# Matmul with batch norm over all rows: two column blocks stored by GpSimd's converting transfers, and the row pieces of two more chunks in halves

## The chip, the cores and the metric

The kernel runs on one core of one Trainium2 chip. The metric is the device time of one execution in microseconds. Before the change it is 205.8 us (median of 3 runs, 205.72 to 206.01).

The engines are named as in the profile: PE is TensorE (PEld is its weight load), DVE is VectorE, ACT is ScalarE, POOL is GpSimd, SP is SyncE, which here only issues DMAs. POOL also issues DMAs, and only those that it issues change the data type on the way.

## The reference

```python
def reference(x, weight, gamma, beta, eps):      # x 16 x 512 x 1024, weight 1024 x 768, f32
    y = np.matmul(x, weight)
    mean = np.mean(y, axis=(0, 1), keepdims=True)
    var = np.var(y, axis=(0, 1), keepdims=True)
    y_norm = (y - mean) / np.sqrt(var + eps)
    return (gamma * y_norm + beta).astype(np.float32)
```

x is 8,192 rows of 1,024 values, 33.5 MB. The output is 8,192 rows of 768 columns, 25.2 MB in f32. Each column is normalised over all rows, so nothing of a column can be stored before the matmuls of that column are done for all rows.

## The kernel before

**Tiles.** The rows are cut into 16 chunks of 512 (`C`). The 768 columns are cut into 6 column tiles of 128 (`NT`), numbered `nt` 0 to 5. Tiles 0 and 1 are the first group (`GA`), computed with rows on the partitions. Tiles 2 to 5 are computed turned, with columns on the partitions and 512 rows per PSUM bank, so their output has to be turned back before it is stored. The "third tile" of the title is `nt = 2`.

**Load stage (about 2 to 100 us).** POOL issues the loads of x (L402) into an SBUF area named `ring`; they convert f32 to bf16. DVE turns each chunk (L434, L427) into `xT_sb`. PE computes the first group of each chunk (L509) and the other tiles of the early chunks (L574). From about 100 us on, everything is in SBUF, and the remaining column tiles run from there at 8 matmuls (L574) for each tile and chunk.

**One column tile and chunk.** PE fills a PSUM bank (`y_ps`, 8 banks in all). DVE reads it for the statistics (L710). ACT casts it to bf16 into `y_sb` (L714), after which the bank is free. For most of tile 2, ACT does both (L719, L723). Where the moving operand is still interleaved, some chunks are first copied into plain order (`x_pl`, L546), by ACT or by DVE: those of chunks 12 to 15 for tile 4 are given to whichever of the two the planner finds free.

**First group, stored by rows (`rows_out`).** A row piece is multiplied by the scale on DVE (L936), the shift is added (L941, on POOL except for five pieces that `ADDED` gives to DVE), and SP stores it (L945). A piece is 4 row tiles of 128 rows (512 KB), except for chunks 0 and 1, which go in two pieces of 2 row tiles (256 KB).

**Tiles 2 to 4, stored in blocks of two chunks (`col_block`).** There are 8 blocks per tile, each 512 KB of output. There are four ways. `MODE` names the way of a block:

- `xact`: the block is normalised in place (L1022 on ACT for tile 2, L1025 on DVE else); SP issues a DMA transpose into a bf16 slot of `ring` (L1219); ACT casts it into an f32 slot (L1231); SP stores that (L1201).
- `xpool`: as far as the transpose the same; then POOL issues one DMA that reads the bf16 slot, converts, and writes the f32 output (L1225). No cast, no f32 slot, no store by SP. Before the change no block takes this way.
- `pe`: PE turns the block (L1043) between other matmuls, ACT copies it out of PSUM (L1209), SP stores (L1201). Tile 4 takes it.
- blocks named in `RAW` (0 and 2 of tiles 2 and 3; 0, 2 and 4 of tile 4, counted in chunks) skip `MODE`: they are transposed raw (L1105), scaled by DVE (L1173), shifted by POOL (L1177), stored by SP (L1181). For them the scale and shift of the tile are spread over the partitions by small copies (L1144: 4 gathers of 32 x 64 and 3 deals of 32 x 256 for each tile, which either POOL or ACT may do) and a copy into PSUM (L1157).

One block of tile 4 is held back to fill the gap before the last tile's scale is known (L1251, L1254).

**The end.** The last matmuls of tile 5 (L752) end its statistics (L759, L1307, L1310, L1322, L1323). DVE then normalises tile 5 (L1347), PE turns it (L1043), ACT copies it out (L1360), and SP stores 4.2 MB (L1363).

**What sets the order.** A planner (`arrange`) takes every task with its own guesses of costs and due times and writes out one fixed order for each engine and DMA queue; each queue then runs in that order and waits by semaphores. The planner also places slots in `ring`, so a slot can be used again only when the store or transpose that read it has landed. An edit of one block's way can therefore move other instructions, between engines too. The first column tile to be finished by `col_block` is tile 2.

Of the kernel before, what the change touches and what calls it, by code (L numbers as in the profile page):

```python
# [227 lines left out]
def kernel(  # L228
# [44 lines left out]
    XT, YB, SQ = C - EARLY, 29, 3  # L273
    ADDED = (0,6,16,28,40)
    PARTED, LATE, SINGLE = (4,5,7,8,9,10), (12,13,14,15), (2,3,6)
    MODE = {2:'xact',3:'xact',4:('pe',)*8}
    MODE = {nt: m if isinstance(m, tuple) else (m,) * (C // GY) for nt, m in MODE.items()}
    RAW, RAWADD, RAWDUE = {2:(0,2),3:(0,2),4:(0,2,4)}, {2:'POOL',3:'POOL',4:'POOL'}, {2:14.0,3:8.0,4:8.0}
    RING = 3 * CH // 32 * KQ // 2
# [75 lines left out]
    def task(prio, engines, emit, deps=(), lock=False, **kw):  # L355
        t = Task(prio, engines, emit, deps, **kw)
        t.lock = lock
        tasks.append(t)
        return t

    def dve(occ):
        return {"DVE": (occ, occ + 0.09)}

    def act(occ):
        return {"ACT": (occ, occ + 0.11)}
# [81 lines left out]
    for kind, n, *n1 in order:  # L447
# [24 lines left out]
        for i in range(rows // QR):  # L472
            c, q = divmod(m0 // QR + i, QPC)
# [9 lines left out]
        if rows % QR:  # L483
            t0 = rows // QR * QR // 32
            m1 = m0 + 32 * t0
            c, q = divmod(m1 // QR, QPC)
# [442 lines left out]
    def rows_out(c, s0, s1, k):  # L929
        due = S + 5.0 + 0.62 * k  # L930
        n = s1 - s0
        slot = Slot(rings, n * NA)

        def norm(eng):
            slot.o = piece(slot).rearrange("p (s n) -> p s n", n=NA)
            seq(nc.vector.tensor_mul(  # L936
                slot.o, y_row[c].y[:, s0:s1], aff[0][:, None, :].to_broadcast([P, n, NA])))

        def add(eng):
            row = sum1[:, 0:NA] if eng == "POOL" else aff[1]  # L940
            seq(ENG[eng].tensor_add(slot.o, slot.o, row[:, None, :].to_broadcast([P, n, NA])))  # L941

        def store(eng):
            m0 = c * CH
            seq(nc.sync.dma_start(  # L945
                out_flat[m0 + s0 * P:m0 + s1 * P, 0:NA].rearrange("(s p) n -> p s n", p=P), slot.o))

        keeps = [row_end[k][3] for k in row_end if k[0] == c]
        a = task(due, dve(0.3 * n), norm, [p0] + keeps, takes=[slot], uses=[y_row[c], a0_slot])
        b = task(due + 0.4, dve(0.3 * n) if k in ADDED else pool(0.59 * n), add, [a, p1 if k in ADDED else sh],  # L950
                 uses=[slot, a1_slot] if k in ADDED else [slot])
        task(due + 1.0, {"SP": (0.38, 0.4)}, store, [b], dma=n * NA * P * 4 / 1024 / 365.0 * 1.024,
             uses=[slot])

    k = 0
    for c in range(RC):
        for s0_, s1_ in ((0, 2), (2, 4)) if c < 2 else ((0, 4),):
            rows_out(c, s0_, s1_, k)
            k += s1_ - s0_

# [57 lines left out]
    def norm(nt, c, n=1):  # L1018
        def emit(eng):
            part = y(nt, c, n)  # L1020
            if eng == "ACT":
                seq(nc.scalar.activation(  # L1022
                    part, part, AF.Identity, bias=shift[:, nt:nt + 1], scale=scale[:, nt:nt + 1]))
            else:
                seq(nc.vector.tensor_scalar(  # L1025
                    part, part, scale[:, nt:nt + 1], shift[:, nt:nt + 1],
                    op0=ALU.mult, op1=ALU.add))
        return emit

    def turn_block(prio, nt, m0, count, deps, uses):  # L1030

        bank = Slot(banks)
        todo = []

        def step():
            if not todo:
                o_ps = psum.tile([P, count, P], bf16, tag="b")
                bank.tile = o_ps
                for s in range(count):
                    c, i = divmod(m0 // P + s, RT)  # L1040
                    todo.append((o_ps[:, s], y(nt, c)[:, i * P:(i + 1) * P]))
            dst, src = todo.pop(0)
            seq(nc.tensor.transpose(dst, src, ident))  # L1043

        def emit(eng):
            for _ in range(emit.task.count):
                step()

        emit.step = step
        t = task(prio, pe(0.0555 * count), emit, deps, takes=[bank], uses=uses)  # L1050
        emit.task = t
        turns[t] = [count, count]
        return t, bank
# [136 lines left out]
    def col_block(nt, c, due, fin_task, held=False):  # L1190
# [12 lines left out]
        a = task(due, act(1.144) if nt == GA else dve(0.45), norm(nt, c, GY), [fin_task] + keeps, nt > GA, uses=[yslot])  # L1203
        if MODE[nt][c // GY] == "pe":
            b, bank = turn_block(due + 0.5, nt, m0, count, [a], [yslot])
# [11 lines left out]
        def xbar(eng):  # L1217
# [3 lines left out]
        b = task(due + 0.5, {"SP": (1.4, 1.4)}, xbar, [a], dma=XBAR,  # L1221
                 takes=[t_slot] + ([slot] if MODE[nt][c // GY] == "xact" else []), uses=[yslot])
        if MODE[nt][c // GY] == "xpool":
            def store_x(eng):
                seq(nc.gpsimd.dma_start(dst(), t_slot.o))  # L1225
# [185 lines left out]
```

## Time and profile before

| | |
|---|---|
| time, median of 3 | 205.8 us (205.72 to 206.01) |
| the profiled execution | 205.96 us, of which the span shown is 204.2 us and 1.76 us lie around it |
| granted TensorE clock | mean 0.975; 1.00 in each stretch looked at between 112 and 190 us |
| busy: PE, DVE, ACT, POOL | 191.0, 158.7, 146.6, 126.1 us |
| HBM read, written | 36.71 MB, 25.17 MB |

How to read it: the page's second part cuts the span in 40 slices of 5.1 us, each digit a busy share in tenths. A row of groups gives the line, engine, operation, out<-in, shapes and count, then busy us and mean ns of one, then the idle time just before these instructions and who ended it. In a timeline a row starts with its start in us and its length in us. In a table of windows, the columns are the stretch, then busy us (and count) of PE, PEld, DVE, ACT and POOL, the granted clock, the mean busy share of the DMA engines and the GB/s moved.

### The profile page before, as it was taken

How to read it: one execution, taken by the hardware profiler on the slowest of the kernel's cores; microseconds unless marked ns; L12 is line 12 of the kernel's file. 1: busy time of each engine (PE TensorE's matmuls, PEld its weight loads, DVE VectorE, ACT ScalarE, POOL GpSimd, SP SyncE). 2: the span in 40 equal slices, each digit the busy share in tenths (PEclk: the TensorE clock that was granted, in tenths of full speed). 3: DMA queues.
4: the chain of work that ended last, by engine and by line, in shares of the span. 5: the costliest groups of instructions: out<-in, count | busy, mean ns of one | idle time of the engine just before them, and what ended most of it. 6: DMA issues, size and time to landing. Idle time of an engine off the chain costs nothing.

```text
span 204.2 us, 3509 instructions
## 1 busy us (share of the span) xinstructions
PE 191.0 (94%) x1210; PEld 116.3 (57%) x1210; DVE 158.7 (78%) x248; ACT 146.6 (72%) x261; POOL 126.1 (62%) x151
## 2 busy tenths in 40 slices
PE   7989999999999999999999999999999999996910
PEld 3467565656588888777875444444444445544810
DVE  4031979989999999969989998977999777937900
ACT  2001461468989999999978766999998969856950
POOL 7776964777399989997403999289616502850000
PEclk9999999999999999999999999999999999999685
DMA  4999999999999999999689999899999999999998
GB/s 73 168 200 196 181 196 196 196 198 197 189 194 197 197 199 194 196 197 195 93 187 214 334 339 336 242 306 326 316 291 201 334 322 244 347 343 310 309 347 249
DMA packets 98562, 48.74 MB, mean 239 GB/s; under 512 B 24304, under 2 KB 98032, under 8 KB 98544
## 3 DMA queue, kind: packets, MB, share of 16 engines
q0 software_dynamic: 34624, 18.36, 65.3%
q1 hardware_dynamic: 63920, 30.16, 53.7%
q8 instruction: 9, 0.15, 0.3%
q14 instruction: 9, 0.07, 0.1%
HBM read 36.71 MB, written 25.17 MB: 303 GB/s over the span
## 4 chain that ended last, share of the span: by engine, by line
PE 86%; ACT 3%; DMA 3%; POOL 2%; issue 1%; ACTq 0%; DVE 0%; POOLq 0%
PE y_ps L574 54%; PE y_ps L509 24%; PE y_ps L813 4%; ACT o_sb L1360 3%; DMA ring<-in_x_dram 3%; PE o_ps L1043 1%; POOL ring L402 1%; POOL w_sb L386 1%; PE y_ps L752 1%; PE a_ps L902 1%; PE o_ps L1073 0%; ACTq L1406 0%; PE idle_ps L590 0%; PE tot_ps L870 0%; ACT ring L1251 0%
## 5 line engine op out<-in xcount | busy, mean ns | idle before, releaser
L574 PEld LDWEIGHTS <-w_sb 128*128 128x128 bf16 x520 | 50.3, 97 | 57.6
L574 PE MATMUL y_ps<-xT_sb,w_sb 128*128 128x512 bf16 (+1 forms) x272 | 59.3, 371 | 0.0
L574 PE MATMUL y_ps<-x_pl,w_sb 128*128 128x512 bf16 x248 | 57.4, 379 | 0.0
L402 POOL DMA_DIRECT2D ring<-in_x_dram x76 | 47.3, 626 | 14.3 <-DMA ring<-in_x_dram 5.3
L509 PE MATMUL y_ps<-w_sb,xT_sb 128*128 128x256 bf16 x448 | 50.6, 273 | 0.7 <-DMA ring<-in_x_dram 0.6
L509 PEld LDWEIGHTS <-xT_sb 128*128 128x128 bf16 x448 | 43.5, 98 | 8.6 <-DVE xT_sb L434 2.1
L434 DVE STREAM_TRANSPOSE xT_sb<-ring 128x1024 f32<-128x1024 f32 (+1 forms) x29 | 31.2, 1112 | 14.1 <-DMA ring<-in_x_dram 14.0
L710 DVE BATCH_NORM_STATS2 stats<-y_ps 128x6 f32<-128x512 f32 x46 | 30.9, 687 | 8.6 <-PE y_ps L574 8.4
L546 ACT COPY x_pl<-xT_sb 128x1024 bf16<-128x1024 bf16 x34 | 34.8, 1063 | 1.7 <-DVE xT_sb L434 1.7
L714 ACT CAST y_sb<-y_ps 128x512 bf16<-128x512 f32 x51 | 28.7, 595 | 8.5 <-DVE stats L710 4.7
L941 POOL TENSOR_TENSOR ring<-ring,sum 128x1024 f32<-128x1024 f32 (+1 forms) x11 | 23.7, 2180 | 15.0 <-ACT y_ps L723 10.8
L658 ACT ACTIVATE sq_sb<-y_ps 128x512 f32<-128x512 f32 x28 | 16.4, 611 | 16.9 <-PE y_ps L509 16.4
L665 POOL TENSOR_TENSOR sum<-sum,sq_sb 128x512 f32<-128x512 f32 x20 | 25.6, 1280 | 3.1 <-ACT sq_sb L658 1.9
L661 DVE TENSOR_TENSOR sum<-y_ps,sum 128x512 f32<-128x512 f32 x28 | 18.9, 675 | 6.4 <-ACT sq_sb L658 5.3
L671 ACT CAST y_sb<-y_ps 128x512 bf16<-128x512 f32 x28 | 16.3, 593 | 8.3 <-DVE sum L661 8.0
L1177 POOL TENSOR_TENSOR ring<-ring,sum 128x1024 f32<-128x1024 f32 x7 | 17.1, 2469 | 4.5 <-issue 2.7
L936 DVE TENSOR_TENSOR ring<-y_sb,a_ps 128x1024 f32<-128x1024 bf16 (+1 forms) x16 | 16.7, 1080 | 0.1
L1144 POOL COPY sum<-sum 32x256 f32<-32x256 f32 (+1 forms) x17 | 5.5, 325 | 16.0 <-ACT sum L1144 9.2
L1043 PE MATMUL o_ps<-ident,y_sb 128*128 128x128 bf16 x104 | 13.7, 249 | 1.6 <-DVE y_sb L1347 1.5
L427 DVE STREAM_TRANSPOSE xT_sb<-ring 128x2048 bf16<-128x2048 bf16 x6 | 13.5, 2290 | 0.2 <-DMA ring<-in_x_dram 0.2
L1231 ACT CAST ring<-ring 128x1024 f32<-128x1024 bf16 x12 | 12.6, 1060 | 0.6 <-DMA ring<-y_sb 0.5
L590 PE MATMUL idle_ps<-idle_sb 128*128 128x512 f32 x18 | 10.5, 741 | 1.5 <-DVE idle_sb L316 1.5
(104 smaller groups left out, 154.9 us busy)
## 6 DMA issues: line engine op xcount, KB each, us to landing
out_dram<-ring SPq DMA_DIRECT2D x37, 512.0 KB, 3.5
ring<-in_x_dram POOLq DMA_DIRECT2D x52, 256.0 KB, 8.9
out_dram<-o_sb SPq DMA_DIRECT2D x6, 512.0 KB, 4.8
ring<-in_x_dram POOLq DMA_DIRECT2D x16, 128.0 KB, 5.8
w_sb<-in_weight_dram POOLq DMA_DIRECT2D x8, 192.0 KB, 6.2
out_dram<-ring SPq DMA_DIRECT2D x6, 256.0 KB, 3.1
ring<-in_x_dram POOLq DMA_DIRECT2D x4, 192.0 KB, 7.8
out_dram<-o_sb SPq DMA_DIRECT2D x3, 256.0 KB, 2.6
```

The source lines that it names most:

```text
L402: bi = seq(nc.gpsimd.dma_start(x_bf[32 * i:32 * i + 32], src[:, :, KQ * i:KQ * (i + 1)]))
L434: seq(nc.vector.transpose(dst, src[:, :, jw0:jw1]))
L509: seq(nc.tensor.matmul(y_ps[:, s], x_of(c, jw, e, t * P, (t + 1) * P), w_sb[:, jw, e, 0:NA], start=(s == 0 and jw == 0 and e == 0), stop=( ...
L546: seq(nc.scalar.copy(dst, pairs) if eng == "ACT" else ENG[eng].tensor_copy(dst, pairs))
L574: seq(nc.tensor.matmul(y_ps, w_sb[:, jw, e, nt * P:(nt + 1) * P], moving(c, jw, e, q0 * QR, q1 * QR, parted), start=(jw == 0 and e == 0 an ...
L661: seq(nc.vector.tensor_add(sum1, slot.tile[:, 0:n], sum1))
L665: seq(ENG[eng].tensor_add(acc, acc, state["sq"][:, 0:n]))
L710: seq(nc.vector.bn_stats(dst, slot.tile))
L714: seq(nc.scalar.copy(y(nt, c), slot.tile))
L936: seq(nc.vector.tensor_mul(slot.o, y_row[c].y[:, s0:s1], aff[0][:, None, :].to_broadcast([P, n, NA])))
L941: seq(ENG[eng].tensor_add(slot.o, slot.o, row[:, None, :].to_broadcast([P, n, NA])))
L1177: seq(ENG[eng].tensor_add(slot.o, slot.o, row[:, None, :].to_broadcast([P, n, P])))
```

## The change

Two edits. In `MODE`, which names the way for each of the 8 blocks of a tile, blocks 2 and 4 of tile 2 (chunks 4 and 5, 8 and 9) become `xpool`; blocks 0 and 1 of that tile are raw either way. In the loop over row pieces, chunks 2 and 3 of the first group go in two pieces each as chunks 0 and 1 do.

```diff
-    MODE = {2:'xact',3:'xact',4:('pe',)*8}
+    MODE = {2:('xact','xact','xpool','xact','xpool','xact','xact','xact'),3:'xact',4:('pe',)*8}
...
     for c in range(RC):
-        for s0_, s1_ in ((0, 2), (2, 4)) if c < 2 else ((0, 4),):
+        for s0_, s1_ in ((0, 2), (2, 4)) if c < 4 else ((0, 4),):
             rows_out(c, s0_, s1_, k)
             k += s1_ - s0_
```

The code of the `xpool` way, there already:

```python
        if MODE[nt][c // GY] == "xpool":
            def store_x(eng):
                seq(nc.gpsimd.dma_start(dst(), t_slot.o))

            task(due + 1.2, {"POOL": (0.93, 0.93)}, store_x, [b], dma=1.69, uses=[t_slot])
```

In the order that is built from the two kernels, PE's instructions are the same, one for one. The others differ from about the seventh row piece of DVE on:

| line | what | before | after |
|---|---|---|---|
| L1231 | cast 128 x 1024, ACT | 12 | 10 |
| L1201 | store 512 KB, SP | 16 | 14 |
| L1225 | converting store, POOL | 0 | 2 |
| L936 | multiply 128 x 1024 / 128 x 512, DVE | 12 / 4 | 10 / 8 |
| L941 | add 128 x 1024 / 128 x 512, POOL | 9 / 2 | 7 / 6 |
| L945 | store 512 / 256 KB, SP | 12 / 4 | 10 / 8 |
| L546 | copy to plain order, ACT / DVE | 34 / 6 | 31 / 9 |
| L1144 | gathers 32 x 64, ACT / POOL | 4 / 8 | 8 / 4 |
| L1144 | deals 32 x 256, ACT / POOL | 0 / 9 | 9 / 0 |

The two L1225 stand on POOL with one whole L941 add between them and one behind them, ahead of four L1177.

## The prediction

> **What bounds the kernel now.** First the page: span, busy times, granted clock, and the groups that the edit touches.
>
> ```profile
> span 204.2 us, 3509 instructions
> PE 191.0 (94%) x1210; PEld 116.3 (57%) x1210; DVE 158.7 (78%) x248; ACT 146.6 (72%) x261; POOL 126.1 (62%) x151
> ...
> PEclk9999999999999999999999999999999999999685
> ...
> L574 PE MATMUL y_ps<-xT_sb,w_sb 128*128 128x512 bf16 (+1 forms) x272 | 59.3, 371 | 0.0
> L402 POOL DMA_DIRECT2D ring<-in_x_dram x76 | 47.3, 626 | 14.3 <-DMA ring<-in_x_dram 5.3
> L546 ACT COPY x_pl<-xT_sb 128x1024 bf16<-128x1024 bf16 x34 | 34.8, 1063 | 1.7 <-DVE xT_sb L434 1.7
> L941 POOL TENSOR_TENSOR ring<-ring,sum 128x1024 f32<-128x1024 f32 (+1 forms) x11 | 23.7, 2180 | 15.0 <-ACT y_ps L723 10.8
> L1231 ACT CAST ring<-ring 128x1024 f32<-128x1024 bf16 x12 | 12.6, 1060 | 0.6 <-DMA ring<-y_sb 0.5
> ```
>
> PE is busy for 94% of the span, L574 has no idle time before it, and the clock is full until slice 38. The chain that ended last is 86% PE. So from about 100 us to the last matmul (186.65 us in the chain) the time is PE's own, and no relief on ACT, POOL or SP shortens it. Whatever the edit saves there is worth nothing; it can only cost, by making PE wait, or change the end behind PE. The table of windows shows the DMA engines over both stretches:
>
> ```profile
> 172.00:174.00 2.00, 2.00 (x17) 1.16 (x16) 1.41 (x3) 2.00 (x4) 0.00 (x0) 1.00 0.70 213
> 174.00:176.00 2.00, 2.00 (x16) 1.07 (x14) 2.00 (x4) 2.00 (x4) 1.59 (x1) 1.00 1.15 346
> ...
> 188.00:190.00 2.00, 1.33 (x15) 0.82 (x16) 1.96 (x7) 1.48 (x5) 0.00 (x0) 1.00 0.89 269
> 190.00:192.00 2.00, 2.00 (x24) 1.74 (x23) 2.00 (x8) 2.00 (x4) 0.00 (x0) 0.66 0.84 253
> ```
>
> 346 GB/s is full rate. They last run short at 172 to 174 us, are then full to about 187, and are short again at 188 to 192: the backlog is gone before the last tile's stores begin (L1363, 189.35 us). The tail hangs on the end of PE, not on the queue. Last, the timeline and the waits of the engine that stands closest behind PE, DVE:
>
> ```profile
> 145.85 0.54 DVE L992 SCALAR_TENSOR_TENSOR tmp<-mv,gamma_sb 128x1 f32<-128x1 f32 x1
> ...
> 153.58 0.70 DVE L710 BATCH_NORM_STATS2 stats<-y_ps 128x6 f32<-128x512 f32 x1 [0.44 <-PE y_ps L574]
> ...
> 160.56 0.70 DVE L710 BATCH_NORM_STATS2 stats<-y_ps 128x6 f32<-128x512 f32 x1 [1.03 <-PE y_ps L574]
> ...
> 164.02 0.70 DVE L710 BATCH_NORM_STATS2 stats<-y_ps 128x6 f32<-128x512 f32 x1 [0.78 <-PE y_ps L574]
> ...
> 168.09 0.53 DVE L1025 TENSOR_SCALAR y_sb<-y_sb,scale,shift 128x1024 bf16<-128x1024 bf16 x1
> ```
> ```profile
> DVE ring L1173 <- DMA out_dram<-ring: 0.8, 1, 0.8
> ```
>
> The brackets are DVE's rest time: 0.44 + 1.03 + 0.78 = 2.25 us, in which it waits for PE and so has caught up. At 168.62 us the L1025 ends that I take the first hosted transpose (PEld L1043, 169.00 us) to need: 0.38 us more. So DVE may lose about 2.6 us between 150 and 164 us before PE feels it. The last line shows the way in: L1173, in DVE's fixed order, already once waits for a store to free its place in `ring`, and behind it stand the statistics (L710), then ACT's cast (L714), then the bank that PE wants.
>
> **The change, part by part.**
>
> *Two casts and two SP stores go.* ACT loses 2 x 1.06 = 2.1 us (L1231), SP two issues of about 0.4 us. Off PE's path: nothing gained in time.
>
> *Two converting stores come, on POOL.* No such store is in this trace. Issue: the nearest row is L402, 626 ns for 512 pieces; this one has 1,024, so 0.63 to 1.25 us, and I take 0.95. Transfer: the x loads move and convert as many values (131,072 each) and the GB/s row holds 196 in the load stage, so 262,144 B / 196 GB/s = 1.34 us; a plain store of the same bytes in the same 1,024 pieces of 512 B takes 524,288 B / 346 GB/s = 1.51 us. If pieces set the price it is 2 x 1.34 = 2.68 us. I take 1.5, the plain store's, as its written side is the same; the range keeps 1.34 to 2.68. By that value the DMA engines do the same work as before.
>
> *Who stands behind them.* POOL waits in order for the transpose (median 4.4 us to landing); behind it are one add (L941) after each, then the L1177. Behind those adds SP's L945 waits (its waits on L941 are 11.5 us in 9 already), and behind L945 the next transposes. POOL has cover: 3.58 us of idle before the L941 at 131.22 us, and the copies leave it. Two issues and about 1 us of waiting on landings come to 2.9 us: inside that.
>
> *Small copies change sides.* POOL loses 4 gathers of 0.23 and 9 deals of 0.39 us, 4.4 us; ACT gains 4 x 0.24 + 9 x about 0.38 (the 128 x 256 copy L1157) = 4.4 us, and gives 3 copies L546 (3 x 1.06 = 3.2 us) to DVE. ACT in sum: -2.1 + 4.4 - 3.2 = -0.9 us. It is busy for all of 128 to 144 us, and five L714 stand in one row at 161.54 us, so up to five of 8 banks were full then; one more holds the spread scale. Two free banks at 1.73 us each are some 3 us of cover (an estimate from these rows), and ACT's net load falls.
>
> *DVE gets more.* Three L546 at 0.69 us = 2.1 us, between 137 and 160 us, against room of 2.6: 0.5 us is left. This is the tightest place. If that cover is gone, each further us on DVE is one on PE.
>
> *Halves.* Two L936 of 1.21 become four of 0.68: +0.3 us on DVE near 115 us, covered by the 0.93 us that DVE idles at 125.7. Two L941 of 2.38 become four of 1.27: +0.3 us on POOL. SP issues two stores more, 2 x 0.37 us, waiting on POOL anyway. The store after the first half starts some 1.2 us sooner; DMA has room there, so nothing.
>
> *The tail.* SP's list behind 165 us holds the same stores of tile 4. A store that slips past 172 us costs 1.51 us of backlog, of which (346 - 269 + 346 - 253) / 346 x 2 = 0.98 us is idle room at 188 to 192. With two stores off SP's queue I expect none to slip.
>
> Sum: PE 0, tail 0. The profiled 205.96 us (204.2 + 1.76 around it) is 0.16 above the median; in the median's terms 205.8 + 0 = 205.8.
>
> **The rivals.**
>
> *Slower, the converting store is dear.* At 2.68 us two of them push the stores that free `ring` by 2 x 1.17 = 2.3 us, L1173's wait grows by that, DVE has 0.5 to spare, PE loses 1.8: 207.6 us. Halfway, about 206.7. It decides from 0.25 us extra on each. For it: the wait in the last fence. Against: loads of x convert at full read rate, and other stores can pass in the meantime. Chance 0.24.
>
> *Slower, DVE is held by POOL.* L992 took 0.54 us above, 0.16 elsewhere, and ended at 146.39, when POOL's L1177 ended (146.36). If a moved L546 starts beside an add of 2.38 us it may stand for all of it: 2.4 - 0.5 = 1.9 us, 207.7; half of it, 206.5. Against: in 143 to 154 us only one of six L546 ran long (0.92 for 0.69), though the adds were there. The Trainium skill (SBUF — State Buffer, "Who interferes with whom") states this as an exclusive lock for the whole instruction, with issue order deciding who blocks; L992's end agrees. The same page, in "SBUF: two separate sides", speaks against the change itself: it says that descriptors of GpSimd's DMAs cannot be written while such a DVE operation runs. No run here shows it, since L402 has no such copy beside it; by its 620 against 3,100 ns (an estimate from that page) each issue would be 2.5 us longer. Chance of this rival 0.12, and 0.02 for PE being held elsewhere.
>
> *Faster.* Only the idle 0.98 us at 188 to 192 could be won, if less backlog let the tail's stores begin sooner: 205.8 - 0.5 = 205.3, at most 204.8. Against: L1360 begins at 188.96 behind DVE and PE, and the first store follows it. Chance 0.10.
>
> *The change doesn't do what it says.* The built order holds both L1225, so no.
>
> **How the numbers follow.** Forecast 0.52, dear store 0.24, port 0.12, elsewhere 0.02, faster 0.10. 0.2% (0.41 us) is about what a measurement of this kernel can tell from no change. So faster 0.10, same 0.52, slower 0.24 + 0.12 + 0.02 = 0.38. The forecast's own range is 205.5 to 206.1. For 8 in 10 I go up to 207.0, over the halfway values of both slower rivals, leaving out their upper ends, and down to 205.4.
>
> **What would show it.** Right: L574 still with 0.0 idle, the last L752 ending near 186.65, the rows at 188 to 192 as now; L1225 below 1.3 us of issue, landing about 4 us after issue; PE's waits without L1043 or L574. Wrong: idle on PE behind DVE or ACT at 140 to 175 us, a wait of L1173 on out_dram over 2 us (dear store), L546 over 1 us beside an add (port), or 346 GB/s through 188 to 192 (backlog).

## The result, and the profile after

| | before | after |
|---|---|---|
| time, median of 4 (same chip) | 205.76 us (205.67 to 206.01) | 208.30 us (208.19 to 208.59) |
| ratio | | 1.0124, 95% interval 1.0106 to 1.0141 |
| span of the profiled execution | 204.2 us | 206.6 us |
| end of the last matmul L752 | 186.65 us | 188.18 us |
| first store of tile 5 (L1363): issued, landed | 189.35, 191.53 us | 190.88, 193.99 us |

The change costs 2.5 us; the forecast of 205.8 us and the range up to 207.0 were wrong. In the span the loss has two parts: the matmuls end 1.53 us later, and the first store behind them takes 0.93 us longer to land (3.11 for 2.18 us). First two lines of the page before, the chain and the statistics on DVE, then the page after: span, engines, chain, the same statistics and the converting stores.

```profile
PE 86%; ACT 3%; DMA 3%; POOL 2%; issue 1%; ACTq 0%; DVE 0%; POOLq 0%
...
L710 DVE BATCH_NORM_STATS2 stats<-y_ps 128x6 f32<-128x512 f32 x46 | 30.9, 687 | 8.6 <-PE y_ps L574 8.4
```

```profile
span 206.6 us, 3520 instructions
...
PE 190.0 (92%) x1210; PEld 115.9 (56%) x1210; DVE 163.6 (79%) x253; ACT 147.1 (71%) x269; POOL 124.3 (60%) x142
...
PE 62%; DVE 12%; DMA 9%; ACT 8%; issue 2%; POOL 2%; ACTq 0%; DVEq 0%; POOLq 0%
...
L710 DVE BATCH_NORM_STATS2 stats<-y_ps 128x6 f32<-128x512 f32 x46 | 30.3, 684 | 4.0 <-PE y_ps L574 4.0
...
out_dram<-ring POOLq DMA_DIRECT2D x2, 512.0 KB, 5.6
```

PE's share of the chain has gone from 86% to 62%, DVE has entered with 12%. DVE is busy for 4.9 us more, and rests 4.0 us in front of L710 where it rested 8.4 us before. The two converting stores land 5.6 us after their issue (median). Next the timeline of DVE and POOL from the second converting store on; a row is start, length, engine, line.

```profile
136.64 0.91 POOL L1225 DMA_DIRECT2D out_dram<-ring  x1
...
136.71 4.38 DVE L546 COPY x_pl<-xT_sb 128x1024 bf16<-128x1024 bf16 x2
...
137.56 2.37 POOL L941 TENSOR_TENSOR ring<-ring,sum 128x1024 f32<-128x1024 f32 x1
...
142.90 2.35 POOL L1177 TENSOR_TENSOR ring<-ring,sum 128x1024 f32<-128x1024 f32 x1 [2.97 <-DVE ring L1173]
...
143.95 1.85 DVE L546 COPY x_pl<-xT_sb 128x1024 bf16<-128x1024 bf16 x1
...
147.60 2.37 POOL L1177 TENSOR_TENSOR ring<-ring,sum 128x1024 f32<-128x1024 f32 x1 [2.35 <-DVE ring L1173]
...
149.09 0.90 DVE L992 SCALAR_TENSOR_TENSOR tmp<-mv,gamma_sb 128x1 f32<-128x1 f32 x1
```

Two copies took 4.38 us. The first one's own record is 136.71 to 140.49 us: 3.78 us where a free copy takes 0.68, ending 0.56 us after POOL's add (139.93). The third took 1.85 us and ended 0.55 us after the L1177 beside it. Then L992 took 0.90 us, where it takes 0.16 alone, and ended with the next L1177. That is 3.1 + 1.2 + 0.7 = 5.0 us of DVE time lost in 13 us. What follows from it is in the timelines of DVE and PE and in the windows:

```profile
158.21 1.22 DVE L1173 TENSOR_TENSOR ring<-r_sb,a_ps 128x1024 f32<-128x1024 bf16 x1 [1.23 <-DMA out_dram<-ring]
...
170.14 0.53 DVE L1025 TENSOR_SCALAR y_sb<-y_sb,scale,shift 128x1024 bf16<-128x1024 bf16 x1
```
```profile
170.73 0.23 PE L1043 MATMUL o_ps<-ident,y_sb 128*128 128x128 bf16 x1 [1.50 <-DVE y_sb L1025]
```
```profile
148.00:150.00 2.00, 2.00 (x12) 0.88 (x10) 2.00 (x5) 2.00 (x5) 1.97 (x1) 1.00 0.00 0
...
174.00:176.00 2.00, 2.00 (x17) 1.17 (x16) 0.58 (x1) 1.98 (x5) 0.00 (x0) 1.00 0.72 216
...
188.00:190.00 2.00, 0.63 (x10) 0.44 (x8) 1.47 (x6) 1.66 (x5) 0.00 (x0) 1.00 1.10 333
190.00:192.00 2.00, 1.80 (x20) 1.13 (x20) 2.00 (x8) 1.50 (x5) 0.00 (x0) 1.00 1.00 302
```

The L1025 that the prediction names (168.09 us before) begins at 170.14, and PE stands for 1.50 us before its first hosted transpose. Between 148 and 150 us the DMA engines move nothing at all (316 GB/s before): SP stands at a store L1201 whose cast on ACT (L1231) ends only at 149.33 us, and ACT had waited 2.0 us for DVE between 141 and 146 us. The last short stretch lies at 174 to 176 us instead of 172 to 174, and at 188 to 192 us, where before had 269 and 253 GB/s, the queue is now busier.

### The profile page after: what moved, and what is told of

Same layout as the page of the kernel before. It is cut to its first block, busy times and chain, and to the rows that moved or that the text cites. A ratio compares the mean times of both kernels' runs of the same rounds, so it can differ in the third digit from the quotient of the medians.

```text
span 206.6 us, 3520 instructions
## 1 busy us (share of the span) xinstructions
PE 190.0 (92%) x1210; PEld 115.9 (56%) x1210; DVE 163.6 (79%) x253; ACT 147.1 (71%) x269; POOL 124.3 (60%) x142
## 4 chain that ended last, share of the span: by engine, by line
PE 62%; DVE 12%; DMA 9%; ACT 8%; issue 2%; POOL 2%; ACTq 0%; DVEq 0%; POOLq 0%
PE y_ps L574 34%; PE y_ps L509 21%; DMA w_sb<-in_weight_dram 6%; DVE stats L710 4%; PE y_ps L813 4%; ACT o_sb L1360 3%; DMA ring<-in_x_dram 3%; DVE x_pl L546 3%; DVE ring L1173 2%; PE o_ps L1043 2%; ACT x_pl L546 1%; DVE y_sb L1025 1%; ACT y_sb L714 1%; POOL ring L402 1%; ACT sum L1144 1%
## 5 line engine op out<-in xcount | busy, mean ns | idle before, releaser
L710 DVE BATCH_NORM_STATS2 stats<-y_ps 128x6 f32<-128x512 f32 x46 | 30.3, 684 | 4.0 <-PE y_ps L574 4.0
L546 ACT COPY x_pl<-xT_sb 128x1024 bf16<-128x1024 bf16 x31 | 31.8, 1055 | 2.0 <-DVE xT_sb L434 1.7
L941 POOL TENSOR_TENSOR ring<-ring,sum 128x1024 f32<-128x1024 f32 (+1 forms) x13 | 24.1, 1880 | 14.6 <-ACT y_ps L723 10.8
L1177 POOL TENSOR_TENSOR ring<-ring,sum 128x1024 f32<-128x1024 f32 x7 | 17.1, 2452 | 19.7 <-DVE ring L1173 15.6
L936 DVE TENSOR_TENSOR ring<-y_sb,a_ps 128x1024 f32<-128x1024 bf16 (+1 forms) x18 | 16.8, 972 | 0.0
L1043 PEld LDWEIGHTS <-y_sb 128*128 128x128 bf16 x104 | 8.8, 112 | 4.5 <-DVE y_sb L1025 2.0
L590 PE MATMUL idle_ps<-idle_sb 128*128 128x512 f32 x18 | 9.6, 685 | 1.5 <-DVE idle_sb L316 1.5
L1231 ACT CAST ring<-ring 128x1024 f32<-128x1024 bf16 x10 | 10.4, 1049 | 0.6 <-DMA ring<-y_sb 0.6
```

Source lines behind the costliest of these rows:

```text
L546: seq(nc.scalar.copy(dst, pairs) if eng == "ACT" else ENG[eng].tensor_copy(dst, pairs))
L710: seq(nc.vector.bn_stats(dst, slot.tile))
```

## The experiments

The theory after the result: DVE's copies L546 are **held** while POOL works (theory A). The rivals: DVE simply has too much work (B, **load**); the stores on POOL keep places of `ring` too long (C, **ring**). "Before" below is the kernel before, run on the same chip. The edits of experiments 1 to 4 are made in the changed kernel, those of experiment 5 in the kernel before. The second edit of experiment 1 takes the `xpool` blocks back, which leaves the kernel before with the halves.

**1. One part of the change alone.** The third tile is `nt` 2, the one with the `xpool` blocks.

```diff
-        for s0_, s1_ in ((0, 2), (2, 4)) if c < 4 else ((0, 4),):
+        for s0_, s1_ in ((0, 2), (2, 4)) if c < 2 else ((0, 4),):
```

> Only the first part of the change: blocks 2 and 4 of the third tile stored by GpSimd's converting transfers; the row pieces stay as before. Theory A (hold): a copy L546 on DVE that meets an add of POOL stands for as long as POOL works. The first L546 of the changed kernel (136.71 us, 3.78 us long) does not depend on the row halves, so A expects a copy of 3 us or more near 137 us again, PE's wait at L1043 of about 1.5 us, and 208.0 to 208.5 us. Theory B (load): DVE has too much work after 130 us, whoever disturbs it. Less work by 0.3 us without the halves: 207.9 to 208.3. Theory C (ring): the two stores keep places of ring too long, L1173 waits for them and DVE is late by that; the stores are the same, so 208.0 to 208.5. If the halves alone are at fault, 205.8.

Measured: 208.20 us, ratio 1.0104 (1.0067 to 1.0141). The first copy took 3.79 us again.

```diff
-    MODE = {2:('xact','xact','xpool','xact','xpool','xact','xact','xact'),3:'xact',4:('pe',)*8}
+    MODE = {2:'xact',3:'xact',4:('pe',)*8}
```

> Only the second part: row pieces of chunks 2 and 3 in halves, the third tile's blocks cast by ScalarE and stored by SP as before. A, B and C all expect 205.7 to 206.0 us, PE's last L752 ending near 186.65 us, and no copy L546 over 1 us. Above 206.5 the halves have a part in the loss.

Measured: 206.21 us, ratio 1.0006 (0.9991 to 1.0021); L752 ended at 186.39 us. The halves cost nothing that can be measured; the loss belongs to the two blocks. A, B and C remain.

**2. The same work in a form that is not held.** Same order on every engine; three copies are written as a maximum over one element.

```diff
-    pending = []
+    pending, one_port = [], [1, 1, 1]
...
-                seq(nc.scalar.copy(dst, pairs) if eng == "ACT" else ENG[eng].tensor_copy(dst, pairs))
+                seq(nc.scalar.copy(dst, pairs) if eng == "ACT" else nc.vector.tensor_reduce(dst, pairs[:, :, :, None], axis=mybir.AxisListType.X, op=ALU.max) if eng == "DVE" and one_port and one_port.pop() else ENG[eng].tensor_copy(dst, pairs))
```

> The changed kernel with its first three DVE copies L546 (at 136.7, 140.4 and 143.9 us) written as a reduction over one element, which gives the same values. The order of every engine is unchanged. The new form costs more by itself: an estimate of 1.1 to 1.2 us each from L936 (1.20 us for 1,024 values of a partition), against 0.69 for an unhindered copy, so +1.3 us of work on DVE. A (hold): if the hold is a matter of the copy's form and the new form is free of it, the three take 1.1 to 1.2 us each although POOL's adds run beside them, DVE wins 6.3 - 3.5 = 2.8 us against the changed kernel, PE's idle time before L1043 at 169 us goes, and the time is 205.8 to 206.3. If the new form is held too, the first stands for 3.8 us again and the time is about 208.3 or more. B (load): DVE carries 1.3 us more work than in the changed kernel: 208.3 to 209.5. C (ring): the stores and L1173's places are the same: 207.5 to 208.5, and L1173 waits for out_dram as long as before or longer.

Measured: 205.94 us, ratio 0.9995 (0.9978 to 1.0012). Its timeline:

```profile
136.75 2.33 DVE L546 TENSOR_REDUCE x_pl<-xT_sb 128x1024 bf16<-128x1024 bf16 x2
...
137.60 2.37 POOL L941 TENSOR_TENSOR ring<-ring,sum 128x1024 f32<-128x1024 f32 x1
...
140.88 2.39 POOL L1177 TENSOR_TENSOR ring<-ring,sum 128x1024 f32<-128x1024 f32 x1 [0.91 <-DVE ring L1173]
...
141.93 1.20 DVE L546 TENSOR_REDUCE x_pl<-xT_sb 128x1024 bf16<-128x1024 bf16 x1
```

Each takes 1.20 us with POOL's add beside it. Without a hold these three would cost DVE 1.6 us more than three free copies of 0.68 us, and yet the whole loss is gone. B and C fall: the load was larger, and the stores were the same and landed as late (5.3 and 5.9 us after their issue). The Trainium skill (SBUF — State Buffer, "Who interferes with whom") says of this reduction that on trn2 it never contends with GpSimd, and of copies that they can; both agree with these rows.

**3. Which POOL instruction holds the copy.** First the add behind the second L1225 is left out:

```diff
-            seq(ENG[eng].tensor_add(slot.o, slot.o, row[:, None, :].to_broadcast([P, n, NA])))
+            seq(ENG[eng].tensor_add(slot.o, slot.o, row[:, None, :].to_broadcast([P, n, NA]))) if k != 52 else None
```

> The changed kernel without the last L941 on POOL, the one that stands behind the second L1225 (137.56 us): the shift of one row piece (chunk 13, first half) is left out. Which POOL instruction holds the copy at 136.71 us: the issue of L1225 (136.64 to 137.55 us), the add behind it (137.56 to 139.93 us), or both? In the changed kernel the copy ended 0.56 us after the add. If the issue holds DVE as well, the copy now ends 0.56 us after the issue, about 1.4 us long. If only adds hold it, and the copy lost its place to the add that came later, it takes 0.69 us. A (hold): DVE gains 2.4 or 3.1 us against the changed kernel, and the time falls to 205.8 to 206.5. B (load): DVE has no instruction less; 208.3. C (ring): only the store of the row piece comes 2.4 us sooner; 207.5 to 208.3.

Measured: 206.16 us, ratio 1.0011 (0.9994 to 1.0027).

```profile
136.43 1.23 POOL L1225 DMA_DIRECT2D out_dram<-ring  x1
...
136.51 1.65 DVE L546 COPY x_pl<-xT_sb 128x1024 bf16<-128x1024 bf16 x2
```

The first copy took 0.68 us, the second 1.05, ending 0.49 us after the issue; the issue itself took 1.23 instead of 0.91 us. So an issue and a copy do get in each other's way, but for tenths of a us. Yet this copy began 13 ns after an add had ended, that of the changed kernel in the same ns; it could have been a matter of who asks first. So the add ahead was shortened, to let the copy ask in the middle of the issue:

```diff
-            row = sum1[:, 0:NA] if eng == "POOL" else aff[1]
-            seq(ENG[eng].tensor_add(slot.o, slot.o, row[:, None, :].to_broadcast([P, n, NA])))
+            row, m = sum1[:, 0:NA] if eng == "POOL" else aff[1], 3 if k == 48 else n
+            seq(ENG[eng].tensor_add(slot.o[:, :m], slot.o[:, :m], row[:, None, :].to_broadcast([P, m, NA])))
```

> The changed kernel with the last L941 but one on POOL (134.34 to 136.71 us) shortened to three quarters: the shift of a quarter of one row piece (chunk 12) is left out. It ends about 0.55 us sooner, at 136.15 us, and the second L1225 issues from about 136.1 to 137.0 us; the copy L546 on DVE still asks at 136.7 us, now in the middle of that issue, with the full add L941 behind it at 137.0 to 139.4 us. Two ways in which the hold could work. H1: whoever asks while POOL still computes loses its turn to POOL's next add too; in the changed kernel the copy began in the same hundredth of a us in which an add ended. Then the copy now gets through in 0.7 us, makes the issue longer by some 0.3 us (1.23 for 0.91 us without the add behind it), and the time is 205.8 to 206.3. H2: an issue followed by an add keeps the copy out anyway. Then the copy ends 0.56 us after the full add, at about 139.9 us, 3.2 us long, and the time is 207.5 to 208.5.

Measured: 207.09 us, ratio 1.0050 (1.0030 to 1.0070).

```profile
136.13 0.91 POOL L1225 DMA_DIRECT2D out_dram<-ring  x1
...
136.74 3.84 DVE L546 COPY x_pl<-xT_sb 128x1024 bf16<-128x1024 bf16 x2
...
137.06 2.37 POOL L941 TENSOR_TENSOR ring<-ring,sum 128x1024 f32<-128x1024 f32 x1
```

The first copy stood from 136.74 to 139.98 us, 3.24 us, until 0.56 us after the end of the add, which began 0.31 us later than it. That is H2: a copy that meets the issue also waits for the add right behind the issue. The time, 207.09 us, lies between H1's and H2's: PE lost nothing here (L752 at 186.64 us; L1173 waited 0.2 us for its place in `ring`, not 1.23), and the loss of 1.1 us is all behind PE. Experiment 5 takes that up.

**4. Versions in which no copy meets an issue with an add behind it, nothing left out.** The add given to DVE:

```diff
-    ADDED = (0,6,16,28,40)
+    ADDED = (0,6,16,28,40,52)
```

> The changed kernel with the add behind the second L1225 given to DVE (one more number in ADDED), nothing left out. The scheduler then puts 1.2 us more work on DVE, ahead of the first copy L546, and the copies one by one between the L710. Hold theory: POOL has nothing to compute between the issue's end (about 137.5 us) and its first L1177 (about 142 us), so the first two copies take 0.7 to 1.0 us; a third that meets an L1177 takes up to 1.9. DVE loses some 2 us to holds instead of 5 and has 1.2 us more work: 205.8 to 206.8. Load theory (fallen already in the run with the three reductions): 209. If the ring's places mattered, no change against the changed kernel, 208.3.

Measured: 206.23 us, ratio 1.0011 (0.9992 to 1.0029). A second run gave the profile:

> The same kernel as in the run before with the add on DVE, for its profile. Its time was 206.23 us there, so PE should have at most 0.3 us of idle time before L1043 at 169 us. Hold theory: the two copies near 138 to 140 us take 0.7 to 1.0 us each since POOL has only the issue of L1225 beside them and nothing to compute behind it; the third meets an L1177 and takes up to 1.9 us. If one of the first two takes over 2 us, the time is explained otherwise than by the hold.

```profile
136.28 0.91 POOL L1225 DMA_DIRECT2D out_dram<-ring  x1
...
136.85 0.83 DVE L546 COPY x_pl<-xT_sb 128x1024 bf16<-128x1024 bf16 x1
...
138.20 0.67 DVE L546 COPY x_pl<-xT_sb 128x1024 bf16<-128x1024 bf16 x1
```

Again a copy asks in the middle of the issue; with no add behind it, it is through after 0.83 us. The third, beside an L1177, took 1.89. Next, the planner. In both kernels it already keeps a DVE task marked `lock`, which these copies are, apart from POOL's adds (`port`), but not from a DMA that POOL issues. Now it is told that the issue of a converting store occupies POOL as an add does:

```diff
-        elif e == "POOL" and not t.dma:
+        elif e == "POOL" and (t.lock or not t.dma):
...
-        if e == "DVE" and t.lock or e == "POOL" and not t.dma:
+        if e == "DVE" and t.lock or e == "POOL" and (t.lock or not t.dma):
...
-            task(due + 1.2, {"POOL": (0.93, 0.93)}, store_x, [b], dma=1.69, uses=[t_slot])
+            task(due + 1.2, {"POOL": (0.93, 0.93)}, store_x, [b], True, dma=1.69, uses=[t_slot])
```

> The changed kernel, but the scheduler counts the issue of a converting store as a time in which POOL holds DVE's copies off. Nothing is left out; it then lays out POOL, DVE and ACT anew: seven small copies L1144 go back to POOL, and the first DVE copy L546 comes behind the second L1177 instead of at 136.7 us. Hold theory: no copy stands beside the adds behind L1225, so no copy is longer than 1.9 us, PE does not wait for L1025 at 169 us, 205.7 to 206.3. If it is as fast as the kernel before, the stores themselves cost nothing. A result above 207 would mean that the hold is only moved, to the copies beside the L1144 and L1177 on POOL.

Measured: 206.04 us, ratio 1.0001 (0.9983 to 1.0020). No DVE copy is longer than 0.82 us, PE's share of the chain is 80%, and the two L1225 land 5.4 and 5.8 us after their issue, as in the changed kernel. So two converting stores cost nothing here, and they gain nothing: no version beats the kernel before.

**5. The tail.** In the kernel with the shortened add PE ends as before, yet the end is 1.0 us later (span 205.2 us). Windows of before, then of that kernel; the last two columns are the DMA engines' mean share and GB/s.

```profile
187.75:188.25 0.50, 0.00 (x0) 0.00 (x0) 0.41 (x3) 0.50 (x2) 0.00 (x0) 1.00 0.49 142
```
```profile
187.75:188.25 0.50, 0.00 (x0) 0.00 (x0) 0.42 (x3) 0.50 (x2) 0.00 (x0) 1.00 1.14 344
...
203.00:203.90 0.90, 0.00 (x0) 0.00 (x0) 0.00 (x0) 0.00 (x0) 0.00 (x0) 0.50 0.07 22
```

Before, the queue runs nearly empty around 188 us. Here it does not, and the last 0.9 us of transfers has a share of 0.07, what one engine of 16 has (1.15 is the share at full rate). To see whether this is a matter of bytes (T1) or of one late engine (T2), the kernel before was given more to store:

```diff
-            seq(ENG[eng].dma_start(dst(), slot.o))
+            for s in (count, 4) if (nt, c) == (4, 12) else (count,): seq(ENG[eng].dma_start(dst()[:, :s], slot.o[:, :s]))
```

> The kernel before, with half of one store of tile 4 (the L1201 issued at 182.19 us) made a second time: 256 KB, 0.75 us at 346 GB/s, with the same data to the same place. Nothing else is changed. The question is the 0.9 to 1.0 us that the shortened add and the changed kernel lose behind PE's end. In the run with the shortened add the DMA engines did not run short at 187.8 to 188.8 us as they do before (share 0.49 and 0.58 there), and its last packets (203.0 to 203.9 us, 22 GB/s, share 0.07) are those of about one engine of 16. T1 (bytes): the tail is late by what exceeds the idle room of 0.98 us at 188 to 192 us. Then 0.75 us more costs nothing: 205.8 to 206.1. T2 (one late engine): a DMA engine is about 1.1 us behind the others since the instruction fetches at about 180 us, and catches up only where the queue runs empty before the last tile's stores. Then a queue that has 0.2 us of pause left instead of 0.98 leaves most of that debt: 206.5 to 207.1, the last 0.7 to 1.1 us of the transfers at about 20 GB/s, and the first L1363 landing about 3 us after its issue instead of 2.18.

> The kernel before, with that whole store made a second time: 512 KB, 1.51 us, the same data to the same place. T1 (bytes): 1.51 less the idle room of 0.98 is 0.5 us: 206.3 to 206.6. T2 (one late engine): 0.5 us for the bytes and some 1.1 us of the debt, since no pause is left: 207.2 to 207.9, with the last 1.1 us at about 20 GB/s. In both, PE's last L752 ends near 186.65 us as before.

Measured: 208.53 us, ratio 1.0127 (1.0096 to 1.0159), and, with the whole store (`(count, count)`), 209.40 us, 1.0171 (1.0141 to 1.0202): above both theories. The second store, to the same place, was issued only when the first had landed (187.47 us for half, 188.31 for the whole), and SP with all stores behind it stood still. As a test of bytes they failed. But windows of the run with the whole store show what looks like one late engine by itself:

```profile
186.00:187.00 1.00, 1.00 (x14) 0.81 (x11) 0.53 (x2) 0.61 (x3) 0.00 (x0) 1.00 0.50 149
187.00:188.00 1.00, 0.07 (x2) 0.00 (x0) 0.73 (x5) 1.00 (x3) 0.00 (x0) 1.00 0.07 20
```

With nothing new in the queue, one engine's share (0.07) goes on alone until about 188 us, after the others have run out by about 186.5 to 187; the store lands at 188.29. In the second try the extra store goes to a scratch area (4 of the 8 row tiles for half, 8 for the whole):

```diff
+    spare = nc.dram_tensor("spare", (1024, 128), f32, kind="Internal").ap().rearrange("(s p) n -> p s n", p=P)
...
-            seq(ENG[eng].dma_start(dst(), slot.o))
+            for d, s in ((dst(), 8), (spare, 4))[:1 + ((nt, c) == (4, 12))]: seq(ENG[eng].dma_start(d[:, :s], slot.o[:, :s]))
```

> As the last two runs were meant, without their flaw (there the second store waited for the first to land, and SP with it, so the queue stood empty for some 2 us at 186 to 188.5 us): the kernel before, and behind the L1201 issued at 182.19 us half of the same block is stored once more, to a scratch area of its own. 256 KB more, 0.75 us at 346 GB/s; no wait is added. T1 (bytes): it fits in the idle room of 0.98 us at 188 to 192 us; no change, 205.8 to 206.2. T2 (one late engine): the run before showed a stretch of about 1.5 us, 186.7 to 188.3, in which about one DMA engine alone was busy, finishing a store of which the others' parts were done; the tail then ended together. A queue that does not run empty before the last tile's stores keeps that engine late to the end: 206.6 to 207.3, with some 1 us at the end of the transfers at about 20 GB/s.

> The same with the whole block stored a second time: 512 KB, 1.51 us. T1 (bytes): 1.51 - 0.98 = 0.5 us more: 206.3 to 206.6. T2 (one late engine): 0.5 us and 1.0 to 1.5 us of the late engine: 207.4 to 208.0, again with about 1 us at 20 GB/s at the end. PE's last L752 ends as before in both.

Measured: 207.28 us, ratio 1.0067 (1.0046 to 1.0087), and 208.01 us, 1.0094 (1.0064 to 1.0124). By bytes it would have been 0 and 0.5 us more; it is 1.3 and 2.1. The first lies in T2's range, the second 0.01 us above it. Windows of the first, then one of the second:

```profile
187.75:188.25 0.50, 0.00 (x0) 0.00 (x0) 0.38 (x2) 0.50 (x3) 0.00 (x0) 1.00 1.15 348
...
202.80:203.80 1.00, 0.00 (x0) 0.00 (x0) 0.00 (x0) 0.00 (x0) 0.00 (x0) 0.50 0.08 23
```
```profile
204.00:205.00 1.00, 0.00 (x0) 0.00 (x0) 0.00 (x0) 0.00 (x0) 0.00 (x0) 0.50 0.06 18
```

T1 falls and T2 is borne out: with half a store PE ends at 186.71 us, the queue does not run empty at 188 us, and one engine's share ends the transfers alone. With the whole store PE ended 0.4 us later in the profiled execution (187.05 us), so not all of its 2.1 us lie in the tail. That it is the same engine each time is not shown, since the trace does not name the engine of a packet. The changed kernel ends in the same way (204.4 to 205.2 us: share 0.07, 21 GB/s).

## Why the prediction was wrong

**The failed step: "DVE is held by POOL".** The prediction had the mechanism, and the sign by which to know it ("L546 over 1 us beside an add"), but gave it 0.12 and at most 207.7 us; in the forecast's sum, "PE 0", it stood at nothing. "Three L546 at 0.69 us = 2.1 us" was the charge; DVE's first three took 3.78, 0.68 and 1.85 us, 6.3 in all. The low chance came from a misreading. "Against: in 143 to 154 us only one of six L546 ran long, though the adds were there." They were not there:

```profile
131.22 4.68 POOL L941 TENSOR_TENSOR ring<-ring,sum 128x1024 f32<-128x1024 f32 x2 [3.58 <-DVE ring L936]
...
135.37 0.58 DVE L1140 COPY sum<-scale 128x32 f32<-128x32 f32 x1
...
141.19 5.17 POOL L1177 TENSOR_TENSOR ring<-ring,sum 128x1024 f32<-128x1024 f32 x2
...
143.23 0.92 DVE L546 COPY x_pl<-xT_sb 128x1024 bf16<-128x1024 bf16 x1
...
147.76 2.09 DVE L546 COPY x_pl<-xT_sb 128x1024 bf16<-128x1024 bf16 x3
...
150.37 0.68 DVE L546 COPY x_pl<-xT_sb 128x1024 bf16<-128x1024 bf16 x1
```

This is the timeline of before: the two L1177 end at 146.37 us, and four of the six copies stand in POOL's pause behind them (its next instruction comes at 152.0). The one copy that met an add did run long, and so did an instruction that the prediction passed over: the small copy L1140 at 135.37 us took 0.58 us, where the same copy takes 0.17 to 0.22 elsewhere, and ended 0.05 us after the L941. The row that speaks against a collision has to be one in which the two engines work at once. The kernel's text held a sign too: its planner keeps these copies apart from POOL's adds. The price was wrong as well: one add less 0.5 us of cover. The first copy waited for an issue and an add, 3.1 us, a second collision took 1.2 and L992 0.7.

**"0.5 us is left. This is the tightest place."** The place was right, the size was not. Only the idle times from 150 us on were counted; the copies come in from 136.7 us, and the timeline of before has 1.03, 0.76 and 0.16 us more at 138 to 141 us. DVE's busy time on the page is 160.6 us with the reductions and 163.2 with the shortened add, 1.9 and 4.5 us more than before, and in neither run did a matmul wait at this place (with the shortened add a weight load waited 0.4 us). So the cover was about 4.5 us, where the prediction had 2.6; the changed kernel, with 4.9 us more, went past it. Where the whole of that cover lies was not followed up.

**From the hold to PE.** "Each further us on DVE is one on PE" did not hold either. A copy shorter by 0.54 us (the shortened add) saved PE's whole 1.5 us: L1025 began at 168.60 us there, 170.14 in the changed kernel. 0.54 us of that difference is the copy, and about 1.0 is L1173's wait for its place in `ring` (0.2 against 1.23 us). So the wait that the prediction put down to a dear store did grow, though the stores were the same in both. The store that L1173 waits for, an L1201, was issued 0.49 us later in the changed kernel, by the hold, and took 1.06 us longer to land (5.42 for 4.36). Why it took longer is not shown.

**"With two stores off SP's queue I expect none to slip."** They slipped because DVE fed them late: nothing was moved for 2 us at 148 us, and with the reductions, where the hold is gone, 340 GB/s were. The price was wrong as well. "1.51 us of backlog" against "0.98 us idle room" is a sum of bytes; experiment 5 shows that the room is also when one late engine catches up, so 0.75 us of backlog that fits into it costs 1.3. In the changed kernel most engines run out at about 204.3 us, 1.5 us later than before (an estimate from the shares of the windows 202.5 to 203 us before, 0.56, and 204 to 204.5 after, 0.63). That is PE's delay; what comes behind it is the share of one engine.

**Right:** the issue of L1225 (0.95 us predicted, 0.93 and 0.91 measured) and that the converting store is not dear (the planner's version, 1.0001), though it landed 5.6 us after its issue rather than 4; the halves at nothing; nothing gained from the casts saved on ACT. The Trainium skill (SBUF — State Buffer, "SBUF: two separate sides") says that GpSimd cannot write its descriptors while such a copy runs. The runs show a trace of that: the issue was 0.32 us longer with two copies beside it (1.23 for 0.91), not the 2.5 us of the prediction's estimate, and nothing where the copy waited (0.91).

## What to carry to other kernels

Before work is moved to an engine that shares something with another, look up where each of the two will stand in the new order, and price a collision by the whole run of instructions on the other side, an issue and the add behind it together. Evidence that two instructions do not disturb each other counts only from rows in which both run at once. A short pause in a full DMA queue may be worth more than its bytes, if one engine catches up in it.

## What was not expected of the hardware

- A copy that met the issue of L1225 waited for the add behind it too (3.24 us and 3.78 us), and without that add 0.83 us. A copy that met an add had its turn when the add ended, although another add stood behind: in before the copy at 143.23 us ended 0.56 us after the first L1177, and the second L1177 took 2.81 us instead of 2.36. Why the two differ stays open.
- What looks like one DMA engine fell about 0.8 to 1.5 us behind the others, in the changed kernel, in the one with the shortened add and in the runs with more to store. In the kernel with the shortened add, the instruction queues fetch 16 KB and 8 KB at about 180 us, in one packet each, 0.96 and 0.31 us long, which together come near that lateness. The kernel before fetches the same two at about 179 us (0.98 and 0.31 us) and ends without a late engine, having had its pause at 188 us. That these packets make the engine late is argued from their length; the trace does not name the engine of a packet, and it was not tried.
